# A fourth split tile in the weight ring of a hybrid layer, with the tiles that make room for it

## The chip, the cores and the metric

One Trainium2 chip, one of its cores. The time is device microseconds of one execution. TensorE is called PE, VectorE DVE, ScalarE ACT, GpSimd POOL; SP issues the transfers.

## The reference

One layer of a hybrid trunk for two groups of tokens, 128 context tokens and 256 latent ones, that share the weights: 384 tokens (T) of width 2048 (D), all in float32. Cut to what matters:

```python
mod = silu(c) @ w_mod + b_mod                     # 2048 -> 6 x 2048, one row per group
h   = rmsnorm(x, norm_mix_g) * (1 + sc_a) + sh_a
mq, mk, mv, mo, mi, mf, rq, rk, rv, rg, sz, sxbc, sdt, gl = split(h @ w_in)
y_m = head_rmsnorm(mlstm(mq, mk, mv, mi, mf)) * sigmoid(mo)   # both directions, chunks of 128
y_r = head_rmsnorm(retention(rq, rk, rv)) * silu(rg)          # both directions, rope on the latents
y_s = rmsnorm(ssd(silu(conv(sxbc)), sdt) * silu(sz))          # both directions
g   = sigmoid(gl)                                 # three gates of width 2048
x   = x + g_a * ((g[0]*(y_m @ w_br_m) + g[1]*(y_r @ w_br_r) + g[2]*(y_s @ w_br_s)) @ w_out)
h   = rmsnorm(x, norm_mlp_g) * (1 + sc_f) + sh_f
x   = x + g_f * (square(relu(h @ w_ff1)) @ w_ff2)
y   = rmsnorm(x, final_norm_g)
```

The final states of the three scans of the context group are outputs too.

## The kernel before

**Products.** A float32 operand is split into a rounded part and a remainder (`whi`, `wlo` for weights; `hhi`, `hlo` or `yhi`, `ylo` for activations), and each product is made of three: high by high, high by low, low by high. The weights are read once, in units of 512 KB: a unit is a `raw` tile of 128 x 1024, loaded by SP (`emit_raws`, L139), from which ACT rounds `whi` (L88) and DVE subtracts `wlo` (L91). `raw` tiles come from a ring of `RAWB` = 6, split tiles from a ring of `SPB` = 3. On PE an "A" unit is 24 matmuls of 128 x 384 with the weights stationary, a "B5" unit 18 matmuls with 512 columns of weights moving.

**The main loop.** `run_units` goes through a list of 696 units in program order. For unit i it first emits the splits up to unit i + `SPB` - 1 (`emit_splits`), then loads as far as the ring of raws allows, then the products of unit i, one step of background work (`bg_steps`), some of the modulation's multiplications (`pop_mods`), and at last the evacuation of the block before (`flush_evac`). Each engine works through its own instructions in the order in which they are emitted here. 128 of the units are of kind "M": a tile of `w_mod`, which is no work for PE at that place but is multiplied and summed by ACT, DVE and POOL (L339, L348). They stand among the others in the list, and count as a unit where the ring looks ahead. The background work is the scans, written as generators with a `yield` behind each step: the mLSTM's, the SSD's (`s_scan`, once for each of two groups of heads) and retention's.

**The SSD scan.** `s_scan` works over six pairs n of chunk and direction. `load(n)` brings a tile `Cb` of eight heads' decays (L1004) and, from n = 2, a tile `EB` for the carried state (L1008). `decay(n)` makes exponentials of `Cb` on ACT and DVE, `weigh(n)` multiplies the masked scores into `Cb` on DVE and makes `xd` on POOL, `inter(n)` is the part of the carried state (PE, then `ti` on DVE with `EB`), and `outs(c)` multiplies `xd` and `Cb` of both directions of a chunk on PE. The ring of `Cb` has 5 buffers, that of `EB` 2, and `load(n + 2)` stands at the end of step n. `h0`, the state at the start, has a buffer of its own.

**The start stage**, up to about 205 us, makes the modulation of `h` and the first gate in ten groups of one row tile (the first four) or two. Each group has units of two halves; in a half unit (`st_half`) PE makes 8/n/2 products that ACT, DVE or POOL add to `acc` (for odd products with one row tile by a copy `at` on ACT, L533). `st_split(i + 2)` stands at the beginning of a unit's second half; the next group's work (`st_gemv`: PE's product with `w_mod`; `st_vec`: its turn into columns; `st_build`: `hhi`, `hlo` of the next row tiles) stands behind the halves that the table `nxt` names.

**Retention.** `r_evac_qk`, `r_evac_v` and `r_evac_g` evacuate q and k, v, and the gate of a pair of heads. `yhi` is a tile of eight slots from the pool `hl`; `y_split` fills it, and `y_op` hands it to the products.

The longest part of the run, from about 1760 to 2750 us, is the MLP: nothing but units and the modulation's last tiles.

Of the kernel before, what the change touches and what calls it, by code (L numbers as in the profile page):

```python
# [16 lines left out]
T = 384  # L17
# [29 lines left out]
def hybrid_step(ctx: ExitStack, tc: tile.TileContext, cpack, x_prompt, x_sample, c, state_mlstm_C,  # L47
# [3 lines left out]
                final_norm_g, y_prompt, y_sample, new_C, new_n, new_m, new_ret, new_ssd):  # L51
    nc = tc.nc
    act, dve, pool, pe, sp = nc.scalar, nc.vector, nc.gpsimd, nc.tensor, nc.sync
    RAWB, SPB = 6, 3

    class Pool:
        def __init__(self, name, side="left", space=None):
# [20 lines left out]
    def gbank(name="gb"):  # L78
        return psum([128, 512], name, bufs=4, tag="g")
# [7 lines left out]
    def rnd(out, in_, **kw):  # L87
        act.activation(out=out, in_=in_, func=AF.Copy, **kw)  # L88
# [421 lines left out]
        held["w"] -= 1  # L510
        st_pump()

    def st_half(i, half):
        g, u = units[i]
        k0, n = groups[g]
        if half:
            st_split(i + 2)
        wh, wl = wsp[i]
        nc_ = 8 // n
        for c_ in range(nc_ // 2 * half, nc_ // 2 * half + nc_ // 2):  # L520
            p = gbank()[:, 0:T]
            q = slice(128 * c_, 128 * c_ + 128)
            for kk in range(n):
                k = k0 + kk
                mm(p, wh[:, kk, q], hhi[:, k], kk == 0, False)
                mm(p, wh[:, kk, q], hlo[:, k], False, False)
                mm(p, wl[:, kk, q], hhi[:, k], False, kk == n - 1)
            a = acc[:, nc_ * u + c_]
            if g == 0:
                act.copy(out=a, in_=p)  # L530
            elif n == 1 and c_ % 2:
                t = start([128, T], "at", bufs=2)
                act.copy(out=t, in_=p)  # L533
                tt(pool, a, a, t, ALU.add)
            else:
                tt(dve, a, a, p, ALU.add)
                if g == NG - 1:
                    act.activation(out=a, in_=a, func=AF.Sigmoid)
# [32 lines left out]
    def st_m0(g):  # L571
        st_gemv(g, 0)

    nxt = {1: {0: (st_m1, st_m0), 1: (st_vec,), 2: (st_build,)}, 2: {1: (st_m1,), 3: (st_m0,), 4: (st_vec,), 5: (st_build,)}}
    i = 0
    for g, (k0, n) in enumerate(groups):
        if g == 4:
            vr2, vr3 = start([84, 128], "vr2", tag="vr1"), start([16, 128], "vr3", tag="crow")
            load_later(graw[:, :, 16:48], w_in[0, :, SDT:SDT + 32].rearrange("(k p) f -> p k f", p=128))
            load_later(graw[:, :, 0:16], w_in[0, :, MI:MI + 16].rearrange("(k p) f -> p k f", p=128))  # L580
            load_later(cp[:, CW0:], cpack[:, CW0:CW1])
            for o, n_, v in ((0, 8, m_norm_g[0]), (8, 8, r_norm_g[0]), (16, 8, s_norm_g[0]), (72, 12, s_conv_b[0])):
                load_later(vr2[o:o + n_], rows(v))
            load_later(vr2[24:72], s_conv_w[0].rearrange("w (a b) -> (w a) b", b=128))
            load_later(vr3, state_mlstm_n[0, 0].rearrange("d h (t p) -> (d h t) p", p=128))
            for d in range(2):
                load_later(biasv[32 * d:32 * d + 4], colv(m_igate_b[0, d]))
                load_later(biasv[64 + 32 * d:68 + 32 * d], colv(m_fgate_b[0, d]))
                load_later(biasv[32 * d + 16:32 * d + 32], colv(s_dt_bias[0, d]))
                load_later(alog[32 * d + 16:32 * d + 32], colv(s_a_log[0, d]))  # L590
                load_later(m0[32 * d:32 * d + 4], colv(state_mlstm_m[0, 0, d]))
            load_later(lg, r_decay[0].rearrange("d h -> (d h)").partition_broadcast(128))
            for hf in range(2):
                load_later(sdv[64 * hf:64 * hf + 64, 0:8],
                           s_d[0].rearrange("(t e) -> e t", e=2)[hf].partition_broadcast(64))
        if g == NG - 1:
            take_vectors(vr2, vr3)
        for h_ in range(4 * n):
            if g == NG - 1 and h_ in (4, 6):
                g_prep(h_ // 2 - 2)  # L600
            st_half(i + h_ // 2, h_ % 2)
            if later_loads:
                later_loads.popleft()()
            for f in nxt[n].get(h_, ()):
                f(g + 1)
        i += 2 * n

    def h_op(k):
# [382 lines left out]
    def s_scan(g):  # L991
# [7 lines left out]
        def load(n):  # L999
            if n < 6:  # L1000
                c_, d = cd[n]
                t = Cbs[n] = Ps([128, 8, 128], "Cb", bufs=5)
                r0 = 32 * d + 16 + 8 * g
                sp.dma_start(out=t, in_=scr[2, r0:r0 + 8, 128 * c_:128 * c_ + 128].partition_broadcast(128))  # L1004
                if n >= 2:
                    E = Ebs[n] = Ps([128, 4, 128], "EB", bufs=2)
                    for hf in range(2):
                        sp.dma_start(out=E[64 * hf:64 * hf + 64],  # L1008
                                     in_=scr[1, r0 + hf:r0 + 8:2, 128 * c_:128 * c_ + 128].partition_broadcast(64))

        def decay(n):
            c_, d = cd[n]
# [38 lines left out]
            yo = y_s[:, 4 * g:4 * g + 4, q]  # L1051
            tt(dve, yo, yo, r3(p_, 4), ALU.add)

        h0 = Ps([128, 2, 4, 128], "h0")
        hT = Ps([128, 2, 2, 512], "hT")
        for d in range(2):
            for j in range(4):
# [54 lines left out]
        for n in range(8):  # L1112
            if n >= 3 and n % 2:
                outs((n - 3) // 2)
            if n < 6:
                decay(n)
                yield
            if 1 <= n < 7:
                weigh(n - 1)
                if 2 <= n < 6:  # L1120
                    inter(n)
                yield
            load(n + 2)

    def s_evac_z(j):
        def f(ps):
# [18 lines left out]
    def s_end():  # L1145
        p_ = bank()
        mm(p_[:, 0:T], ones, SS["sqs"])
        run_delayed(True)
        P["s"].close()
        P["hl"] = Pool("hl", "right")  # L1150
        Rs = P["Rs"] = P["hl"]([128, T], "Rs")
        act.activation(out=Rs, in_=p_[:, 0:T], func=AF.Sqrt, scale=1.0 / 1024, bias=K("eps")[:, 0:1])
        dve.reciprocal(out=Rs, in_=Rs)
        P["yhi"] = P["hl"]([128, 8, T], "yhi", dt=F32R)
        P["ylo"] = [None] * 8
        P["r"] = Pool("pr", "right")
        r_begin()
        yield
# [49 lines left out]
    def r_evac_qk(p, which):  # L1208
        def f(ps):
            Pr = P["r"]  # L1210
            r_free(p)
            t = Pr([128, 3, 512], which + "tok")
            act.activation(out=t[:, 0], in_=ps[0], func=AF.Copy, scale=1.0 if which == "q" else 128.0 ** -0.5)
            for c_ in (1, 2):
                cos, sin = (K(n + which)[:, 64 * c_ - 64:64 * c_] for n in ("cos", "sin"))
                for q in (slice(0, 256), slice(256, 512)):
                    t1, t2 = Pr([128, 4, 64], "rt1"), Pr([128, 4, 64], "rt2")
                    s4 = ps[c_][:, q].rearrange("p (a b) -> p a b", b=64)
                    tt(dve, t1, s4, bcast(cos, 1, 4), ALU.mult)
                    tt(dve, t2, s4, bcast(sin, 1, 4), ALU.mult)  # L1220
                    o4 = t[:, c_, q].rearrange("p (h x b) -> p h x b", h=2, x=2)
                    t1v, t2v = (x.rearrange("p (h x) b -> p h x b", x=2) for x in (t1, t2))
                    tt(pool, o4[:, :, 0], t1v[:, :, 0], t2v[:, :, 1], ALU.subtract)
                    tt(pool, o4[:, :, 1], t1v[:, :, 1], t2v[:, :, 0], ALU.add)
            for i in range(2):
                heads.setdefault(2 * p + i, {})[which] = t[:, :, 256 * i:256 * i + 256]
        return f

    def r_evac_v(p):
        def f(ps):  # L1230
            r_free(p)
            t = P["r"]([128, 3, 512], "vtok")
            for c_ in range(3):
                act.copy(out=t[:, c_], in_=ps[c_])
            for i in range(2):
                heads[2 * p + i]["v"] = t[:, :, 256 * i:256 * i + 256]
                bg.append(r_scan(2 * p + i))
        return f
# [106 lines left out]
        yield  # L1345

    def y_split(i, src):
        rnd(P["yhi"][:, i], src)
        if P["ylo"][i] is None:
            P["ylo"][i] = P["hl"]([128, T], "ylo%d" % i, dt=F32R)  # L1350
        tt(dve, P["ylo"][i], src, P["yhi"][:, i].bitcast(F32), ALU.subtract)

    def r_evac_g(p):
        def f(ps):
            while p not in r_done:
                bg_steps(1)
            for i in range(2):
                sg = P["r"]([128, T], "sg", bufs=2)
                act.activation(out=sg, in_=ps[i][:, 0:T], func=AF.Silu)
                tt(pool, sg, sg, RR[2 * p + i], ALU.mult)  # L1360
                later(1, lambda i=i, sg=sg: y_split(2 * p + i, sg))
        return f
# [21 lines left out]


    def y_op(k):
        return P["yhi"][:, k], P["ylo"][k]

    GG = {}

# [357 lines left out]
```

## Time and profile before

| | us |
|---|---|
| median of 3 runs | 2800.89 (2799.49 to 2803.43) |
| the profiled execution, its own time | 2799.41 |
| its span in the trace | 2797.6 |
| PE busy | 2726.8 (97%) |
| DVE busy | 1531.8 (55%) |
| ACT busy | 1122.1 (40%) |
| POOL busy | 638.7 (23%) |

The span is what the trace covers of the profiled execution; the 1.8 us between it and the execution's own time lie around it. Busy time counts the instructions that work, not those that issue transfers or wait. A matmul's record is longer than the distance to the next, since matmuls overlap: what counts is the distance from start to start.

### The profile page before, as it was taken

To read this page: it belongs to the slowest core of one execution; us is meant where nothing else is said; L and a number is where in the kernel's file an instruction comes from. 1 tells how busy PE (TensorE), PEld (TensorE's weight loads), DVE (VectorE), ACT (ScalarE), POOL (GpSimd) and SP (SyncE) were. 2 spreads that over 40 slices of the span, in tenths; PEclk is the share of its full clock that TensorE was granted. 3 is DMA by queue.
4 is the path that set the end of the run, shared out by engine and by line. 5 is a ranking of instruction groups with operands and counts; after the bars stand their busy time and mean duration, and the time that the engine had idled before them with its cause. 6 is when DMAs were issued, how large, how long until landed. Compare 5 with 4: busy or idle time off the path is not lost. (4 is left out here: it accounts for less than half of the span.)

```text
span 2797.6 us, 38171 instructions
## 1 busy us (share of the span) xinstructions
PE 2726.8 (97%) x15109; PEld 2509.8 (90%) x15109; DVE 1531.8 (55%) x1937; ACT 1122.1 (40%) x1656; POOL 638.7 (23%) x534
## 2 busy tenths in 40 slices
PE   8999999999999999999999998999999999999998
PEld 7899989898888888999999987998899899889987
DVE  3666566666546556667558646767334334334434
ACT  5333454546543342443344445544233233323333
POOL 4200233402241111121236422345100100010012
PEclk9999999999999999999999999999999999999999
DMA  9955456466646455666656743666443444344442
GB/s 318 314 187 172 139 174 180 133 184 184 184 120 195 149 168 160 182 180 196 205 183 215 255 155 91 194 190 194 139 128 127 130 128 125 128 130 126 126 144 102
DMA packets 381755, 471.03 MB, mean 168 GB/s; under 512 B 21317, under 2 KB 281049, under 8 KB 380425
## 3 DMA queue, kind: packets, MB, share of 16 engines
q1 hardware_dynamic: 381576, 468.61, 54.2%
q8 instruction: 118, 1.93, 0.3%
q14 instruction: 61, 0.49, 0.1%
HBM read 452.22 MB, written 16.33 MB: 167 GB/s over the span
## 5 line engine op out<-in xcount | busy, mean ns | idle before, releaser
L91 DVE TENSOR_TENSOR wlo<-raw,whi 128x1024 fp32r<-128x1024 f32 x599 | 799.8, 1340 | 953.4 <-ACT whi L88 951.9
L88 ACT ACTIVATE whi<-raw 128x1024 fp32r<-128x1024 f32 x600 | 631.9, 1058 | 987.9 <-PE gb L100 446.3
L100 PE MATMUL gb<-hhi,whi 128*128 128x384 f32 x1600 | 551.4, 345 | 11.3 <-ACT whi L88 5.9
L100 PE MATMUL gb<-hhi,wlo 128*128 128x384 f32 x1600 | 540.0, 337 | 16.7 <-DVE wlo L91 16.5
L100 PE MATMUL gb<-hlo,whi 128*128 128x384 f32 x1600 | 537.4, 336 | 0.4 <-DVE hlo L91 0.4
L100 PE MATMUL gb<-h2l,whi 128*128 128x384 f32 x1024 | 344.5, 336 | 5.1 <-DVE h2l L1555 5.0
L100 PE MATMUL gb<-h2i,whi 128*128 128x384 f32 x1024 | 343.9, 336 | 1.5 <-ACT h2i L1551 1.5
L100 PE MATMUL gb<-h2i,wlo 128*128 128x384 f32 x1024 | 343.4, 335 | 0.0
L100 PEld LDWEIGHTS gb<-hhi,whi 128*128 128x128 f32 x1600 | 302.2, 189 | 27.0 <-issue 9.3
L339 DVE SCALAR_TENSOR_TENSOR macc<-raw,cs,macc 128x512 f32<-128x512 f32 x372 | 319.4, 872 | 7.6 <-DMA macc<-in_b_mod_dram 0.7
L100 PEld LDWEIGHTS gb<-hhi,wlo 128*128 128x128 f32 x1600 | 301.9, 189 | 23.1 <-DVE wlo L91 22.9
L100 PEld LDWEIGHTS gb<-hlo,whi 128*128 128x128 f32 x1600 | 302.0, 189 | 1.7 <-DVE hlo L91 0.7
L91 POOL TENSOR_TENSOR macc<-macc,raw 128x512 f32<-128x512 f32 x140 | 224.7, 1605 | 335.2 <-issue 283.4
L91 POOL TENSOR_TENSOR x<-x,t 128x512 f32<-128x512 f32 x45 | 71.6, 1621 | 735.6 <-DVE t L91 735.6
L100 PEld LDWEIGHTS gb<-h2l,whi 128*128 128x128 f32 x1024 | 193.2, 189 | 8.0 <-DVE h2l L1555 7.9
L100 PE MATMUL gb<-whi,ahi 128*128 128x512 f32 x512 | 199.4, 389 | 0.0
L100 PE MATMUL gb<-whi,alo 128*128 128x512 f32 x512 | 199.3, 389 | 0.0
L100 PE MATMUL gb<-wlo,ahi 128*128 128x512 f32 x512 | 199.2, 389 | 0.0
L100 PEld LDWEIGHTS gb<-h2i,whi 128*128 128x128 f32 x1024 | 193.3, 189 | 2.9 <-ACT h2i L1551 1.9
L100 PEld LDWEIGHTS gb<-h2i,wlo 128*128 128x128 f32 x1024 | 193.3, 189 | 0.0
L100 PE MATMUL gb<-ylo,whi 128*128 128x384 f32 x384 | 128.4, 334 | 0.6 <-DVE ylo L91 0.6
L100 PE MATMUL gb<-yhi,whi 128*128 128x384 f32 x384 | 128.5, 335 | 0.0
(443 smaller groups left out, 3872.7 us busy)
## 6 DMA issues: line engine op xcount, KB each, us to landing
raw<-in_w_in_dram SPq DMA_DIRECT2D x264, 512.0 KB
raw<-in_w_ff_dram SPq DMA_DIRECT2D x256, 512.0 KB
raw<-in_w_mod_dram SPq DMA_DIRECT2D x128, 512.0 KB
mraw<-in_w_mod_dram SPq DMA_DIRECT2D x32, 1024.0 KB
raw<-in_w_out_dram SPq DMA_DIRECT2D x32, 512.0 KB
sg<-scr_g SPq DMA_DIRECT2D x22, 384.0 KB
raw<-in_w_br_r_dram SPq DMA_DIRECT2D x16, 512.0 KB
raw<-in_w_br_m_dram SPq DMA_DIRECT2D x16, 512.0 KB
```

The source lines that it names most:

```text
L88: act.activation(out=out, in_=in_, func=AF.Copy, **kw)
L91: eng.tensor_tensor(out=out, in0=a, in1=b, op=op)
L100: pe.matmul(out, l, r, start=start, stop=stop)
L339: dve.scalar_tensor_tensor(out=macc[:, v], in0=t[:, kk], scalar=cs[:, 2 * r + kk, v:v + 1], in1=macc[:, v], op0=ALU.mult, op1=ALU.add)
```

## The change

The split ring gets a fourth tile of each kind, 8 KB more in a partition. Room comes from three places: the decay tiles `Cb` go from five buffers to four, which `h0` shares, and are loaded two at a time at odd n (for n = 3 behind `outs(0)`); `EB` goes from two buffers to one, loaded behind the `inter` that read it last; and `qtok` and `vtok` of retention take the two buffers in which `yhi` stands later, now as two tiles of four slots, made when the first gate is evacuated. In the start stage the next group's work and the split move from the ends of half units into their middle, and `st_build` in the groups with two row tiles from behind half unit 5 into half unit 6. No engine gets an instruction more or less.

```diff
-    RAWB, SPB = 6, 3
+    RAWB, SPB = 6, 4
...
-    def st_half(i, half):
+    def st_half(i, half, mid):
         g, u = units[i]
         k0, n = groups[g]
-        if half:
-            st_split(i + 2)
         wh, wl = wsp[i]
         nc_ = 8 // n
         for c_ in range(nc_ // 2 * half, nc_ // 2 * half + nc_ // 2):
+            if c_ % (nc_ // 2) == nc_ // 4:
+                for f in mid:
+                    f(g + 1)
+                if half:
+                    st_split(i + 2)
             p = gbank()[:, 0:T]
...
-    nxt = {1: {0: (st_m1, st_m0), 1: (st_vec,), 2: (st_build,)}, 2: {1: (st_m1,), 3: (st_m0,), 4: (st_vec,), 5: (st_build,)}}
+    nxt = {1: {0: (st_m1, st_m0), 1: (st_vec,), 2: (st_build,)}, 2: {1: (st_m1,), 3: (st_m0,), 4: (st_vec,), 6: (st_build,)}}
...
-            st_half(i + h_ // 2, h_ % 2)
+            st_half(i + h_ // 2, h_ % 2, nxt[n].get(h_, ()))
             if later_loads:
                 later_loads.popleft()()
-            for f in nxt[n].get(h_, ()):
-                f(g + 1)
...
-                t = Cbs[n] = Ps([128, 8, 128], "Cb", bufs=5)
+                t = Cbs[n] = Ps([128, 8, 128], "Cb", bufs=4)
                 r0 = 32 * d + 16 + 8 * g
                 sp.dma_start(out=t, in_=scr[2, r0:r0 + 8, 128 * c_:128 * c_ + 128].partition_broadcast(128))
-                if n >= 2:
-                    E = Ebs[n] = Ps([128, 4, 128], "EB", bufs=2)
-                    for hf in range(2):
-                        sp.dma_start(out=E[64 * hf:64 * hf + 64],
-                                     in_=scr[1, r0 + hf:r0 + 8:2, 128 * c_:128 * c_ + 128].partition_broadcast(64))
+
+        def load_e(n):
+            if 2 <= n < 6:
+                c_, d = cd[n]
+                r0 = 32 * d + 16 + 8 * g
+                E = Ebs[n] = Ps([128, 4, 128], "EB")
+                for hf in range(2):
+                    sp.dma_start(out=E[64 * hf:64 * hf + 64],
+                                 in_=scr[1, r0 + hf:r0 + 8:2, 128 * c_:128 * c_ + 128].partition_broadcast(64))
...
-        h0 = Ps([128, 2, 4, 128], "h0")
+        h0 = Ps([128, 2, 4, 128], "h0", bufs=4, tag="Cb")
...
             if n >= 3 and n % 2:
                 outs((n - 3) // 2)
+            if n % 2:
+                load(n + 1)
+                if n == 1:
+                    load_e(2)
+                load(n + 2)
             if n < 6:
                 decay(n)
                 yield
...
                 if 2 <= n < 6:
                     inter(n)
+                    load_e(n + 1)
                 yield
-            load(n + 2)
...
-        P["yhi"] = P["hl"]([128, 8, T], "yhi", dt=F32R)
...
-            t = Pr([128, 3, 512], which + "tok")
+            t = P["hl"]([128, 3, 512], "qtok", bufs=2, tag="yhi") if which == "q" else Pr([128, 3, 512], "ktok")
...
-            t = P["r"]([128, 3, 512], "vtok")
+            t = P["hl"]([128, 3, 512], "vtok", bufs=2, tag="yhi")
...
-        rnd(P["yhi"][:, i], src)
+        yh = P["yhi"][i // 4][:, i % 4]
+        rnd(yh, src)
...
-            while p not in r_done:
+            while p not in r_done or not {2, 3} <= r_read:
                 bg_steps(1)
+            if p == 0:
+                P["yhi"] = [P["hl"]([128, 4, T], "yhi", bufs=2, dt=F32R) for _ in range(2)]
```

How the order moves. First ACT, some units into the main loop, where the first scan of the mLSTM ends; `whi` are the splits, L348 multiplies tiles of the modulation, L905 (L906 in the changed kernel) writes the mLSTM's output. Before:

```order
L893 ACTIVATE jk,sq<-hb 128x256
L88 ACTIVATE whi<-raw 128x1024
L895 ACT_TABLE_LOAD
L895 ACTIVATE sq<-sq,cp 128x3
L88 ACTIVATE whi<-raw 128x1024 x2
L348 ACTIVATE raw<-raw,cs 128x512 x2
L905 ACTIVATE y_m<-sb,vec 128x384 x2
L348 ACTIVATE raw<-raw,cs 128x512 x2
L88 ACTIVATE whi<-raw 128x1024 x2
L792 COPY v_3984<-gb 128x2x256 x2
```

And now:

```order
L894 ACTIVATE jk,sq<-hb 128x256
L88 ACTIVATE whi<-raw 128x1024
L896 ACT_TABLE_LOAD
L896 ACTIVATE sq<-sq,cp 128x3
L88 ACTIVATE whi<-raw 128x1024
L348 ACTIVATE raw<-raw,cs 128x512 x2
L88 ACTIVATE whi<-raw 128x1024
L906 ACTIVATE y_m<-sb,vec 128x384 x2
L88 ACTIVATE whi<-raw 128x1024
L348 ACTIVATE raw<-raw,cs 128x512 x2
L88 ACTIVATE whi<-raw 128x1024
L793 COPY v_3988<-gb 128x2x256 x2
```

Between the two pairs of L348 stood no split, and two behind them; now one stands behind the first pair, one behind `y_m`, one behind the second pair.

SP's queue in the second scan, from the stores of `so` on; L1105, L1004, L1008 and L1178 are L1110, L1005, L1013 and L1187 in the changed kernel. Before:

```order
L1105 DMA out_dram<-so 128x128 x8
L1004 DMA Cb<-scr 128x8x128
L1008 DMA EB<-scr 64x4x128 x2
L139 DMA raw<-in_w_in_dram 128x4x256
L1178 DMA scr_g<-ga__6941 128x384
L1178 DMA scr_g<-ga__6943 128x384
L1004 DMA Cb<-scr 128x8x128
L1008 DMA EB<-scr 64x4x128 x2
L1004 DMA Cb<-scr 128x8x128
L1008 DMA EB<-scr 64x4x128 x2
L139 DMA raw<-in_w_in_dram 128x4x256 x5
```

And now:

```order
L1110 DMA out_dram<-so 128x128 x8
L1005 DMA Cb<-scr 128x8x128
L1013 DMA EB<-scr 64x4x128 x2
L1005 DMA Cb<-scr 128x8x128
L1187 DMA scr_g<-ga__6949 128x384
L1187 DMA scr_g<-ga__6951 128x384
L1013 DMA EB<-scr 64x4x128 x2
L1005 DMA Cb<-scr 128x8x128 x2
L139 DMA raw<-in_w_in_dram 128x4x256 x6
L1187 DMA scr_g<-ga__7132 128x384
L1187 DMA scr_g<-ga__7134 128x384
L1013 DMA EB<-scr 64x4x128 x2
```

The loads of `Cb` come in pairs, and of the loads of `EB` (two halves each) the third now comes behind the raws that it stood ahead of.

ACT in the start stage, around a copy of the modulation (L461), a build (L490 and `hhi`) and the `at` copies (L533, now L536). Before:

```order
L461 COPY macc<-gemv 128x256
L88 ACTIVATE whi<-raw 128x1024
L533 COPY at<-gb 128x384 x4
L490 ACTIVATE ht<-sb,shA,scA 128x128
L490 ACTIVATE ht<-sb,shA,scA 128x256
L88 ACTIVATE hhi<-ht 128x384
L88 ACTIVATE whi<-raw 128x1024
L533 COPY at<-gb 128x384 x4
L461 COPY macc<-gemv 128x256
L88 ACTIVATE whi<-raw 128x1024
```

And now:

```order
L461 COPY macc<-gemv 128x256
L536 COPY at<-gb 128x384 x2
L88 ACTIVATE whi<-raw 128x1024
L536 COPY at<-gb 128x384 x2
L490 ACTIVATE ht<-sb,shA,scA 128x128
L490 ACTIVATE ht<-sb,shA,scA 128x256
L88 ACTIVATE hhi<-ht 128x384
L536 COPY at<-gb 128x384 x2
L88 ACTIVATE whi<-raw 128x1024
L536 COPY at<-gb 128x384 x2
L461 COPY macc<-gemv 128x256
```

The copies stood in fours, with build and split one behind the other; now they stand in pairs, one of the other things between each two.

## Rows read from the trace of the kernel before

**Rows 1.** Page: busy time; xcount | busy, mean ns | idle before it.

```profile
PE 2726.8 (97%) x15109; PEld 2509.8 (90%) x15109; DVE 1531.8 (55%) x1937; ACT 1122.1 (40%) x1656; POOL 638.7 (23%) x534
...
L91 DVE TENSOR_TENSOR wlo<-raw,whi 128x1024 fp32r<-128x1024 f32 x599 | 799.8, 1340 | 953.4 <-ACT whi L88 951.9
L88 ACT ACTIVATE whi<-raw 128x1024 fp32r<-128x1024 f32 x600 | 631.9, 1058 | 987.9 <-PE gb L100 446.3
```

**Rows 2.** Windows: us, busy PE, PEld, DVE, ACT, POOL, PEclk, DMA, GB/s.

```profile
340.00:650.00 310.00, 300.82 (x1663) 282.02 (x1662) 197.53 (x282) 153.92 (x255) 103.69 (x104) 1.00 0.56 167
650.00:1075.00 425.00, 400.24 (x2242) 364.07 (x2241) 249.86 (x331) 186.50 (x297) 101.64 (x104) 0.98 0.56 164
1760.00:2750.00 990.00, 990.00 (x5046) 903.25 (x5045) 451.46 (x452) 344.16 (x426) 161.44 (x98) 1.00 0.46 143
```

**Rows 3.** Waits of PE, 340 to 1265 us: total, times, longest.

```profile
PE gb L100 <- DVE wlo L91: 25.4, 22, 2.9
PE gb L100 <- ACT whi L88: 6.6, 4, 3.5
PE sb L100 <- POOL xd L91: 3.5, 1, 3.5
```

**Rows 4.** Timeline of ACT: start, us, operation xcount [idle before <-releaser].

```profile
413.10 1.33 ACT L348 ACTIVATE raw<-raw,cs 128x512 f32<-128x512 f32 x2
414.32 2.00 ACT L88 ACTIVATE whi<-raw 128x1024 fp32r<-128x1024 f32 x2
```

**Rows 5.** Timeline of PE behind two of the waits.

```profile
417.77 0.45 PE L100 MATMUL gb<-hhi,wlo 128*128 128x384 f32 x1 [0.88 <-DVE wlo L91]
...
1258.19 0.33 PE L100 MATMUL gb<-hlo,whi 128*128 128x384 f32 x1
1259.74 0.44 PE L100 MATMUL gb<-hhi,wlo 128*128 128x384 f32 x1 [1.21 <-DVE wlo L91]
```

**Rows 6.** Timeline of PE, 657 to 662 us.

```profile
657.56 0.44 PE L100 MATMUL gb<-hhi,wlo 128*128 128x384 f32 x1 [2.36 <-DVE wlo L91]
...
658.01 0.52 PE L100 MATMUL gb<-hlo,whi 128*128 128x384 f32 x1
...
661.21 0.42 PE L100 MATMUL gb<-hhi,wlo 128*128 128x384 f32 x1
```

**Rows 7.** Windows at three stretches of lower clock (PEclk third from end).

```profile
657.00:662.00 5.00, 4.44 (x16) 4.45 (x17) 1.66 (x6) 4.97 (x10) 0.00 (x0) 0.66 0.39 105
808.00:812.00 4.00, 3.48 (x30) 3.18 (x31) 0.13 (x1) 0.90 (x2) 3.37 (x4) 0.57 0.48 136
1067.00:1071.00 4.00, 2.90 (x7) 2.32 (x8) 3.96 (x6) 1.25 (x2) 2.42 (x3) 0.57 0.44 123
```

**Rows 8.** Timelines of SP and ACT: a load, and who waits for it.

```profile
1024.04 0.93 SPq L139 DMA_DIRECT2D raw<-in_w_in_dram  x2
...
1028.70 1.06 ACT L88 ACTIVATE whi<-raw 128x1024 fp32r<-128x1024 f32 x1 [0.72 <-DMA raw<-in_w_in_dram]
```

**Rows 9.** Waits of PE, 0 to 340 us.

```profile
PE gb L100 <- ACT at L533: 3.6, 3, 1.8
```

**Rows 10.** Timelines of SP and ACT, second scan; waits of SP.

```profile
750.13 0.38 SPq L1004 DMA_DIRECT2D Cb<-scr  x1
...
754.49 1.28 ACT L1017 ACTIVATE Cb<-Cb,colA 128x128 f32<-128x128 f32 x4 [5.73 <-DMA Cb<-scr]
...
777.94 0.45 SPq L1004 DMA_DIRECT2D Cb<-scr  x1
...
785.23 1.28 ACT L1017 ACTIVATE Cb<-Cb,colA 128x128 f32<-128x128 f32 x4 [0.18 <-DMA Cb<-scr]
...
SPq L1008 <- DVE ti L91: 7.2, 2, 4.8
```

**Rows 11.** Waits of PE, 650 to 810 us.

```profile
PE gb L100 <- DVE wlo L91: 5.4, 4, 2.4
PE gb L100 <- ACT whi L88: 5.4, 2, 3.5
```

More of the change, by code (lines that the diff above doesn't have):

```diff
@@ L1347, in y_split @@
     def y_split(i, src):
-        rnd(P["yhi"][:, i], src)
+        yh = P["yhi"][i // 4][:, i % 4]
+        rnd(yh, src)
         if P["ylo"][i] is None:
             P["ylo"][i] = P["hl"]([128, T], "ylo%d" % i, dt=F32R)
-        tt(dve, P["ylo"][i], src, P["yhi"][:, i].bitcast(F32), ALU.subtract)
+        tt(dve, P["ylo"][i], src, yh.bitcast(F32), ALU.subtract)
     def r_evac_g(p):
         def f(ps):
-            while p not in r_done:
+            while p not in r_done or not {2, 3} <= r_read:
                 bg_steps(1)
+            if p == 0:
+                P["yhi"] = [P["hl"]([128, 4, T], "yhi", bufs=2, dt=F32R) for _ in range(2)]
             for i in range(2):
@@ L1386, in y_op @@
     def y_op(k):
-        return P["yhi"][:, k], P["ylo"][k]
+        return P["yhi"][k // 4][:, k % 4], P["ylo"][k]
     GG = {}
```

## The prediction

> **What bounds the kernel now.** The page comes first: PE is busy for 97% of the span, DVE for 55%, ACT for 40% [rows 1]. So only two things can shorten the run: PE's gaps, and stretches in which PE runs at its lower clock. The windows by stage then show where the gaps are [rows 2]: from 340 to 1075 PE lacks 9.2 and 24.8 us, while from 1760 to 2750 it is busy for 990.00 of 990 us, although the same ring of three split tiles feeds it there. The ring is too short only where other work shares ACT and DVE with it (DVE is busy for 64% from 340 to 650, for 46% from 1760 on).
>
> The waits of PE name the gaps [rows 3]: from 340 to 1265 it waits 22 times for `wlo` (25.4 us) and 4 times for `whi` (6.6 us), once for `xd` (3.5 us). ACT's timeline shows how one arises [rows 4]: two `whi` start at 414.32, right behind multiplications of the modulation's tiles (L348) from 413.10; the subtraction on DVE (1.34 us, [rows 1]) can only follow, and PE goes on at 417.77 [rows 5]. These raws had long landed; the split stood too late in ACT's own order. In the kernel's order, 239 real units of the main loop have but one other real unit between the emission of their split and its use (where a unit of the modulation, which gives PE nothing, takes the place of the second), and all but one of the small waits fall on such units.
>
> A wait costs more than its idle [rows 5]: from 1258.19 to 1259.74 are 1.55 us between two starts that are otherwise 0.17 apart, and only 1.21 of them are idle: 0.16 more for the refill. Last, the clock [rows 6]: behind the wait of 2.36 us at 657.56 the matmuls start 0.32 us apart instead of 0.17, from 658.01 to 661.21; the granted clock of that stretch is 0.66 of full, the lower level, 1.2 of 2.4 GHz, for two thirds of it [rows 7]. There are six such stretches from 650 to 1075, the last at 1067; five follow a wait for a split, the one at 808 the wait for `xd`.
>
> **The change part by part.**
>
> a) *The ring, 3 to 4.* Every split is issued one unit earlier on ACT and DVE. In the new order 222 of the 239 units have two real units in between, 17 still one. One A unit is 24 matmuls at 0.173 = 4.15 us of PE; the longest wait for a split is 3.5 us [rows 3]. So one unit covers each of the waits, if the split moves by its whole unit. The waits are 25.4 + 6.6 = 32.0 us over 26 times, with the refill 32.0 + 26 x 0.16 = 36.2 us. Of these 17/239 stay, 2.6, and I keep 0.6 back for units that gain less than their whole lead: **-33.0 us**. What pays: the raw is wanted a unit earlier. The one landing that shows in full takes 4.66 us, from the issue at 1024.04 to 1028.70 [rows 8]; with `whi` 1.06 and `wlo` 1.34 [rows 1] it makes 7.1 us from issue to use. Two A units are 8.3 us, so I take it as covered (rival B, if not).
>
> b) *The clock.* In that stretch ten steps take 3.20 us where they would take 1.73: 1.5 us lost [rows 6]. Five of six stretches follow a split wait: 5 x 1.5 = **-7.5 us**. Between 0 (the lower level comes for another reason) and -9.
>
> c) *The start stage* (0 to about 205). Vectors, gemv, build and split move from the ends of half units into their middles. PE's waits there for the `at` copies are 3.6 us, three times [rows 9]; the copy now stands ahead of the split in three of the groups with one row tile (1 us of ACT, the length of `whi`), so I take 3 x 1.0 saved, against 1.0 in the first group and some 0.6 where the build now comes half a unit later and is followed at once by its use: **-1**, between -6 (all of the 3.6 with refills, and a little of the gemv's) and +4 (four of the groups lose one `whi` each).
>
> d) *The decay tiles.* The `Cb` ring goes from 5 to 4 and is shared with `h0`; tiles come in pairs, and the second pair's loads wait on SP for PE's `outs`. `EB` has one buffer: its next load waits until DVE has made `ti`. Such waits of SP exist already, 7.2 us over 2 [rows 10]. Behind SP's wait stand raw loads; they were issued many units ahead, and 7 us of delay is not yet seen by PE while raws are two units ahead. A `Cb` lands in 4.36 us (750.13 to 754.49, with ACT idle for 5.73) or at most 7.29 (777.94 to 785.23) [rows 10]; between a load of `EB` and its use stand two background steps, so two units, 8.3 us. By that it is covered, with a margin of 1.0 us. I take **+2**, between 0 and +8 (two holds of the upper kind with half of it covered). "Double-buffer for performance" is a rule of the Trainium skill (page Trainium Kernel Development and Optimization, section Best Practices), so that transfers overlap with compute. It speaks against the single buffer of `EB`; by it each load would stand bare, which is rival D.
>
> e) *`xd`.* The wait for it is untouched (POOL works it, behind ACT's exponentials) and PE arrives there sooner, as the waits ahead of it are gone: **+1.1**, between 0 and +3.5 (as much again, [rows 3]).
>
> f) *What is late next.* Background steps on PE wait for DVE and ACT, which now work nearer to PE. DVE's 64% rises to some 66% when the stretch shortens. From 1760 to 2750 nothing is late [rows 2], so the lower end is 0; the upper is three waits of the longest `wlo` kind, 3 x (2.9 + 0.16) = 9.2, say 10. I take **+2**.
>
> `qtok` and `vtok` in the ring of `yhi` cost nothing: the gate's evacuation now also waits for two more reads, and in the emission no background step has to be forced for them; covered by the steps already made. If that cover went, one step more (4.2 us) would come early, not in addition.
>
> Sum: -33.0 - 7.5 - 1 + 2 + 1.1 + 2 = -36.4 us. The profiled execution took 2799.4 us (span 2797.6 and 1.8 around it): 2763.0. The median of the runs shown is 1.5 above the profiled one, so **2764.5 us**.
>
> **The rivals.**
>
> *B, raws come late.* The raws' own ring stays at six, so a longer split ring takes its unit out of the lead of the raws: in the new order 82 splits, not 29, come right behind the issue of their raw. If each of the 53 more makes ACT wait as at 1028.70, 0.72 us [rows 8], ACT loses 38 us, and what is queued behind it waits too; with half of it on PE, +19: 2764.5 + 19 = 2783. For: the landing is there in the row. Against: ACT is idle for 60% and the margin to use is two units.
>
> *C, nothing moves.* ACT's splits are held by PE anyway: before `whi` ACT was idle for 446.3 us because PE still read the tile [rows 1]. If the ring's length only moves where ACT stands, and each split still meets the same work ahead of it, about 2800. For: the 446 us. Against: they belong mostly to stretches where PE lacks nothing; and by the order, the split of rows 4 moves ahead of the multiplications that held it.
>
> *D, slower: the single `EB` and the pairs.* Each scan makes four loads with no spare buffer (`EB` of 3, 4 and 5, `Cb` of 4), eight for two scans. If what waits for them holds up ACT and DVE for a whole landing, 7.29 us [rows 10], and the splits queued behind, PE loses 8 x 7.3 = 58 us. The stage's own split waits (10.8 us, six times, [rows 11]) and clock stretches would remain, so the gain elsewhere is 32.0 - 10.8 + 20 x 0.16 = 24.4 and two stretches, 3.0. 2799.4 + 58.4 - 27.4 = 2830.4, with the 1.5 **2832 us**. It decides from (27.4 + 5.6)/8 = 4.1 us per hold. For: ACT did wait 5.73 us for a `Cb`. Against: two units lie between.
>
> **How the numbers follow.** A, the sum, 0.73; B 0.17; C 0.06; D 0.04. A's own range is 2752 (clock and start at their good ends, nothing late) to 2782 (c, d, e and f at their bad ends: 5 + 6 + 2.4 + 8 = 21, of which not all at once). The range reaches over B: **2752 to 2786**, which leaves out C, D and a tenth of the rest. About 0.2% (5.6 us) can be told from no change: faster 0.90 (A and B), same 0.06 (C), slower 0.04 (D).
>
> **What would show it.** Right: waits for `wlo` and `whi` from 340 to 1265 under 5 us in all; one clock stretch, behind `xd`; PE's idle from 71 to about 40 us; 1760 to 2750 as before. Wrong: `whi` waiting for DMA of raw often (B); the same waits for `wlo` at other places (C); ACT, DVE or PE waiting for `EB` or `Cb` by DMA, more than 4 us eight times over (D); a stretch at 1.2 GHz without a wait ahead of it (term b).

## The result, and the profile after

The changed kernel takes **2759.93 us** (median of 4 runs, 2758.89 to 2761.18) against 2800.19 (4 runs, 2798.99 to 2803.43) for the kernel before: a ratio of 0.9855, 95% interval 0.9838 to 0.9872. That is 40.3 us less; the forecast was 36.4 less, and 2764.5.

First the page of the changed kernel (parts 1 and 5, as [rows 1]):

```profile
span 2757.7 us, 38218 instructions
...
PE 2714.7 (98%) x15109; PEld 2508.3 (91%) x15109; DVE 1522.9 (55%) x1937; ACT 1122.0 (41%) x1656; POOL 627.0 (23%) x534
...
L88 ACT ACTIVATE whi<-raw 128x1024 fp32r<-128x1024 f32 x600 | 629.8, 1057 | 931.2 <-PE sb L100 385.9
```

PE's work is the same 15109 matmuls; its idle time falls from 70.8 to 43.0 us, and its busy time from 2726.8 to 2714.7 although nothing was taken from it: the longer matmuls at the lower clock and the 0.16 us that a wait costs beyond its idle [rows 5] both count as busy. ACT still idles in front of `whi` for PE, 385.9 us where matmuls into the tiles `sb` release it and 381.2 where those into `gb` do; before it was 445.5 and 446.3, and the page's line in [rows 1] shows only the larger of the two. Next the waits of PE from 225 to 1240 us, the stretch that answers to [rows 3]; columns are total us, times, longest:

```profile
PE sb L100 <- POOL xd L91: 4.8, 2, 3.7
PE sb L100 <- DVE Cb L91: 4.7, 4, 1.9
PE gb L100 <- DVE wlo L91: 1.5, 3, 0.7
```

The 26 waits for splits, 32.0 us, have become three, 1.5 us. In their place stand four waits for `Cb` (0.4 us before) and two for `xd` (one, 3.5). The windows by stage, which answer to [rows 2], and the one stretch at the lower clock that is left between the start stage and the MLP ([rows 7] for those of before):

```profile
339.00:636.30 297.30, 297.30 (x1667) 283.37 (x1666) 194.37 (x282) 155.08 (x257) 103.09 (x104) 1.00 0.58 173
636.30:1039.00 402.70, 391.56 (x2242) 358.06 (x2241) 246.35 (x327) 184.58 (x296) 98.11 (x103) 0.99 0.57 172
1720.00:2710.00 990.00, 990.00 (x5046) 903.27 (x5045) 448.23 (x451) 344.00 (x425) 155.68 (x98) 1.00 0.45 143
783.00:791.00 8.00, 4.65 (x33) 4.32 (x34) 3.67 (x4) 0.90 (x2) 7.37 (x7) 0.57 0.39 125
```

From 339 to 636 PE now lacks nothing of 297.30 us (before: 9.2 of 310); in the next stage 11.1 (24.8); in the MLP the same 990.00 of 990. The six stretches at 1.2 GHz from 650 to 1075 have become one, from 783.8 on, 6.83 us long; it begins within the second of the two waits for `xd` (782.6 to 786.35). The stretch at the MLP's beginning, behind waits for `x` and `h2i`, is there in both kernels (from 1716 for 13.7 us before, from 1678 for 17.1 now), and the start stage has a new one (below). These are the signs that the prediction asked for: under 5 us of waits for splits, one stretch, behind `xd`, about 40 us of idle, the MLP as before.

How the split of [rows 4] now stands on ACT:

```profile
405.99 1.51 ACT L348 ACTIVATE raw<-raw,cs 128x512 f32<-128x512 f32 x2 [3.96 <-DVE macc L339]
409.65 1.06 ACT L88 ACTIVATE whi<-raw 128x1024 fp32r<-128x1024 f32 x1 [2.15 <-PE sb L104]
410.61 1.03 ACT L906 ACTIVATE y_m<-sb,vec 128x384 f32<-128x384 f32 x2
411.54 1.06 ACT L88 ACTIVATE whi<-raw 128x1024 fp32r<-128x1024 f32 x1
412.66 1.51 ACT L348 ACTIVATE raw<-raw,cs 128x512 f32<-128x512 f32 x2
414.08 1.04 ACT L88 ACTIVATE whi<-raw 128x1024 fp32r<-128x1024 f32 x1
```

The `whi` run singly, one behind the first pair of multiplications (409.65), one behind `y_m` (411.54), one behind the second pair (414.08). Before, two of them started at 414.32, and PE waited 0.88 us [rows 5]; now nothing on PE waits there.

### The profile page after: what moved, and what is told of

Its sections match the earlier page's. It is cut to its first block, busy times and chain, and to the rows that moved or that the text cites. A ratio compares the mean times of both kernels' runs of the same rounds, so it can differ in the third digit from the quotient of the medians.

```text
span 2757.7 us, 38218 instructions
## 1 busy us (share of the span) xinstructions
PE 2714.7 (98%) x15109; PEld 2508.3 (91%) x15109; DVE 1522.9 (55%) x1937; ACT 1122.0 (41%) x1656; POOL 627.0 (23%) x534
## 4 chain that ended last, share of the span: by engine, by line
PE 86%; DVE 2%; issue 1%; ACT 1%; DMA 1%; POOL 0%; SPq 0%; DVEq 0%; ACTq 0%; POOLq 0%
PE gb L100 70%; PE sb L100 15%; PE sb L104 1%; DMA raw<-in_w_in_dram 1%; DVE wlo L91 0%; DVE h2l L1567 0%; ACT whi L88 0%; DVE macc L339 0%; DVE Cb L91 0%; POOL y_s L91 0%; POOL y_s L1152 0%; DVE x L91 0%; DMA Cb<-scr 0%; POOL xd L91 0%; ACT h2i L1563 0%
## 5 line engine op out<-in xcount | busy, mean ns | idle before, releaser
L88 ACT ACTIVATE whi<-raw 128x1024 fp32r<-128x1024 f32 x600 | 629.8, 1057 | 931.2 <-PE sb L100 385.9
L339 DVE SCALAR_TENSOR_TENSOR macc<-raw,cs,macc 128x512 f32<-128x512 f32 x372 | 303.7, 829 | 12.2 <-DMA macc<-in_b_mod_dram 2.9
```

The costliest lines, as they stand in the source:

```text
L339: dve.scalar_tensor_tensor(out=macc[:, v], in0=t[:, kk], scalar=cs[:, 2 * r + kk, v:v + 1], in1=macc[:, v], op0=ALU.mult, op1=ALU.add)
```

## The experiments

Times are medians. They stand beside the changed kernel's 2759.93 and, as ratios, beside runs of the kernel before on the same chip (medians 2800.73, 2801.57 and 2801.51 us).

**Is it the ring?** The ring back at three:

```diff
-    RAWB, SPB = 6, 4
+    RAWB, SPB = 6, 3
```

> The changed kernel with the ring of split tiles back at 3, all else as changed. Theory R (the ring pays for everything): the waits for wlo and whi and the stretches at 1.2 GHz come back, 36 and 6 us, and the waits for Cb and xd that the change brought shrink by 2 to 5 us, as PE comes later to them: 2797 to 2803 us. Theory S (the moved order of scans and start stage carries a third or more): below 2787.

Measured: 2799.32 us, ratio to before 0.9995 (0.9986 to 1.0003). Waits of PE, 225 to 1265:

```profile
PE gb L100 <- DVE wlo L91: 24.7, 22, 2.9
PE gb L100 <- ACT whi L88: 6.3, 4, 3.2
PE sb L100 <- POOL xd L91: 3.5, 1, 3.5
PE sb L100 <- DVE Cb L91: 0.4, 1, 0.4
```

Theory R. With three tiles all else in the change is worth nothing that can be measured, and it costs nothing either: with pairs of `Cb`, one `EB` and the new start the waits for `Cb` and `xd` are those of before to a tenth.

**Is it the tile or its place in the order?** Four tiles, but each split emitted where three tiles had it:

```diff
-            emit_splits(i + SPB)
+            emit_splits(i + SPB - 1)
```

> Four split tiles as changed, but a split is emitted at the index at which three tiles had it (one unit later). Theory O (what counts is the place in ACT's and DVE's order; PE's hold on the tile does not matter): the time of the ring of 3, within 5 us, with 20 or more waits for wlo. Theory T (what counts is that the tile is free earlier): within 5 us of the changed kernel, 2755 to 2765.

Measured: 2797.11 us, ratio 0.9988 (0.9980 to 0.9997). ACT's timeline at the place of [rows 4]:

```profile
412.13 1.33 ACT L348 ACTIVATE raw<-raw,cs 128x512 f32<-128x512 f32 x2
413.36 2.00 ACT L88 ACTIVATE whi<-raw 128x1024 fp32r<-128x1024 f32 x2
```

The waits of PE there, 225 to 1265 us:

```profile
PE gb L100 <- DVE wlo L91: 25.0, 23, 2.9
PE gb L100 <- ACT whi L88: 6.6, 4, 3.5
```

Theory O. The pair of `whi` is back behind the multiplications, and the waits for splits with it. A free tile alone gives about 2 us; what the fourth tile is good for is that it allows the split to be put one unit earlier into the queues of ACT and DVE.

**What is the start stage worth?** `st_half`, `nxt` and the loop of the start as before, the rest as changed:

```diff
-                for f in mid:
-                    f(g + 1)
-                if half:
-                    st_split(i + 2)
...
+        if half:
+            st_split(i + 2)
...
+            for f in nxt[n].get(h_, ()):
+                f(g + 1)
```

> The changed kernel with the start stage as before. If the start stage is a zero sum by its waits (copies give 2.4 us, the gemv's load costs 1.6, a new stretch at 1.2 GHz near 30 us costs 3.4): within 1.5 us of the changed kernel, no stretch near 30 us, waits for at copies back at 3.6 us. If the moved order was worth something of its own: 2763 or more; if the stretch is all it brings: 2757 or less.

Measured: 2762.60 us (2760.28 to 2763.24), ratio 0.9861 (0.9846 to 0.9876). The new order is worth 2.7 us by the medians and 1.7 by the ratios (0.9861 and 0.9855). That lies between the first two theories, and the intervals overlap. The waits for the `at` copies are back at 3.5 us, as expected, but two stretches of lower clock appeared at other places (windows, PEclk third from the end):

```profile
21.00:26.00 5.00, 4.51 (x52) 4.24 (x45) 0.47 (x4) 2.86 (x6) 1.39 (x1) 0.71 1.01 268
83.00:88.00 5.00, 4.71 (x18) 4.71 (x19) 3.92 (x6) 2.53 (x4) 4.68 (x4) 0.66 1.08 358
```

The kernel before, with the same order in this stage, had none there; another run with that order (four of each, below) has them from 22 and from 83.5 us on. So what the start stage gives depends in part on stretches whose place the order doesn't set; that stays open.

**Why does PE now wait for `Cb` and `xd`?** `outs(1)` and `outs(2)` one background step later:

```diff
-            if n >= 3 and n % 2:
-                outs((n - 3) // 2)
+            if n == 3:
+                outs(0)
+            elif n == 7:
+                yield
+                outs(2)
...
             if 1 <= n < 7:
+                if n == 5:
+                    outs(1)
                 weigh(n - 1)
```

> The changed kernel with outs(1) and outs(2) of the SSD scan one background step later. Theory L (PE now arrives at outs before weigh and xd are done, one unit is enough): the waits for Cb at 680 and 698 (2.1 and 1.7 us with refill) and for xd at 780 and 782 (5.1) go, and with the last the stretch at 1.2 GHz near 784 (3.1): 2748 us, 2745 to 2752. If the stretch comes without a wait ahead of it: 2751 to 2754. If weigh and xd are simply pushed along with the step (DVE and POOL are behind for more than one unit): 2757 to 2762.

Measured: **2748.09 us** (2747.82 to 2748.41), ratio 0.9812 (0.9799 to 0.9826), the lowest time found, with one other that can't be told apart from it (below). Its waits of PE, 225 to 1265 us:

```profile
PE gb L100 <- DVE wlo L91: 2.1, 4, 0.7
PE sb L100 <- DVE Cb L91: 0.4, 1, 0.4
```

Theory L, with the time worked out for it. Both waits for `xd` and three of four for `Cb` are gone, and no stretch at 1.2 GHz is left between the start stage and the MLP. At the same place as before, around the `outs` that start at 784.43 without a wait, the granted clock (third from the end) is now 1.00:

```profile
783.00:791.00 8.00, 7.99 (x66) 7.33 (x65) 2.90 (x2) 1.25 (x3) 6.99 (x5) 1.00 0.43 129
```

So the stretch at 783.8 came with the waits for `xd`.

**Or do the single `EB` and the pairs hold the scan up?** First two buffers for `EB`:

```diff
-                E = Ebs[n] = Ps([128, 4, 128], "EB")
+                E = Ebs[n] = Ps([128, 4, 128], "EB", bufs=2)
```

> The changed kernel with two buffers for EB (its next load no longer waits for ti). Theory F (PE's new waits for Cb come from PE being earlier, not from the loads): the four waits for Cb, 4.7 us, and the two for xd, 4.8 us, stay, DVE's 1.1 us for EB goes: 2758 to 2761. Theory D (the single buffer holds SP, and what stands behind it): the waits for Cb fall below 2 us, 2752 to 2757.

Measured: 2759.48 us, ratio 0.9851 (0.9835 to 0.9867). Waits of PE:

```profile
PE sb L100 <- DVE Cb L91: 5.2, 4, 1.9
PE sb L100 <- POOL xd L91: 4.8, 2, 3.7
```

Then `Cb` loaded one at a time, in the ring of four:

```diff
-            if n % 2:
-                load(n + 1)
-                if n == 1:
-                    load_e(2)
-                load(n + 2)
+            if n == 3:
+                load(4)
+            if n == 1:
+                load_e(2)
...
                 yield
+            if n != 2:
+                load(n + 2)
```

> The changed kernel with the tiles Cb loaded one at a time again, at the ends of steps 0, 1 and 3 and (that of n = 4) behind outs(0), in the same ring of four. Theory F (PE's new waits come from PE being earlier): waits for Cb 4 to 6 us in 4, for xd 4.8 in 2, 2758 to 2762. Theory P (the pairs hold up SP, ACT or DVE): the waits for Cb fall under 2 us, 2752 to 2757.

Measured: 2759.81 us, ratio 0.9854 (0.9840 to 0.9867); `xd` 4.8 us in 2, `Cb` 3.5 in 3. Both times theory F by the time and by `xd`; the waits for `Cb` without pairs came out somewhat below its 4 to 6 us in 4. Neither the single buffer nor the pairs cost anything that the time shows. The loads have enough ahead of them, although SP in the changed kernel waits longer for `ti` than before (7.2 us in 2, [rows 10]):

```profile
SPq L1013 <- DVE ti L91: 16.8, 5, 6.0
```

**How much lead have the raws left?** Five raws:

```diff
-    RAWB, SPB = 6, 4
+    RAWB, SPB = 5, 4
```

> The changed kernel with five raws instead of six. In it ACT waits 27 times, 77 us in all, for a raw to land (before: 7 times, 16.9 us), and PE sees none of it. Theory M (behind these waits lies more than a unit of reserve, 4.15 us): no wait of PE for whi or wlo above 1 us, 2763 at most. Theory N (less than a unit lies there, so the change has used up the lead of the raws): ten or more of the 27 reach PE with 1 to 4 us each, 2770 to 2790.

Measured: 2768.97 us, ratio 0.9884 (0.9869 to 0.9899): 9.0 slower than the change, between the two theories. ACT's timeline shows a wait for a raw:

```profile
553.32 1.06 ACT L88 ACTIVATE whi<-raw 128x1024 fp32r<-128x1024 f32 x1 [6.10 <-DMA raw<-in_w_in_dram]
```

and PE's timeline what comes of it:

```profile
554.43 0.69 PE L100 MATMUL gb<-hhi,whi 128*128 128x384 f32 x1 [3.85 <-ACT whi L88]
...
556.49 0.52 PE L100 MATMUL gb<-hlo,whi 128*128 128x384 f32 x1
...
560.65 0.52 PE L100 MATMUL gb<-hhi,wlo 128*128 128x384 f32 x1
```

One raw (not ten) reaches PE late, by 3.85 us, and behind it the matmuls start 0.32 us apart for some 6 us: the one wait costs about twice its idle. The rest of the 9.0 goes with it in small waits: `Cb` 6.7 us in 5 (4.7 in 4 before), `wlo` 2.4 in 6 (1.5 in 3). In the rest of the 49 waits of ACT for a raw PE doesn't wait over 1 us for a split, so for all but one the reserve is more than a unit, and for that one less.

**The same ring paid by the raws.** The kernel before with four of each:

```diff
-    RAWB, SPB = 6, 3
+    RAWB, SPB = 4, 4
```

> The kernel before with four split tiles paid by two raws (six to four), all else as before. If the split's place in the order is all that counts: 2760, as changed. If the lead of the raws is as short as theory N has it: two units less cost twice what five raws cost, 2785 to 2830, waits of PE for whi behind DMA of raw.

Measured: 2824.37 us, ratio 1.0078 (1.0063 to 1.0093), slower than before. ACT's wait for raws from 225 to 1240 us:

```profile
ACT whi L88 <- DMA raw<-in_w_in_dram: 186.3, 64, 18.2
```

and waits of PE, for `wlo` from 225 to 1265 us and from 1300 us on, and for the gemv's loads:

```profile
PE gb L100 <- DVE wlo L91: 7.8, 8, 2.5
...
PE gb L100 <- DVE wlo L91: 8.2, 8, 1.8
...
PE gemv L100 <- DMA mraw<-in_w_mod_dram: 10.1, 7, 2.7
```

From 225 to 1265 us two thirds of the wait for `wlo` are away (25.4 to 7.8), but new waits stand there, the longest of 5.3 us for `kT` and 4.1 for `Cb`. The start loses 11 us (there the loads stand in one line, and that of a raw that has to wait holds the next ones), and the MLP, where nothing was late in the kernel before, waits for splits and loses 13 (both by where the same matmuls stand in the two traces: 222.7 against 211.7 us at the end of the start, 25.7 later at the MLP's end against 12.3 at its beginning). The unit of lead has to come from elsewhere than the raws, and that is what the smaller tiles of the scans pay for.

**The first group of the start as before, with `outs` later.**

```diff
-            st_half(i + h_ // 2, h_ % 2, nxt[n].get(h_, ()))
+            st_half(i + h_ // 2, h_ % 2, nxt[n].get(h_, ()) if g else ())
...
+            if g == 0:
+                for f in nxt[n].get(h_, ()):
+                    f(g + 1)
```

> The changed kernel with outs(1) and outs(2) one step later and, in the first group of the start stage, the next group's work at the ends of half units as before. If the gemv's wait for its load (2.5 us near 28) is what the middle costs and what the stretches at 1.2 GHz near 14 and 30 follow: both go, 2744 to 2746. If these stretches come without regard to that order (as in the start stage put back as before, which had two): 2747 to 2749.

Measured: 2747.74 us, ratio 0.9808 (0.9793 to 0.9823), not told apart from 2748.09: the second value. The gemv's waits for its loads come to 4.8 us against 3.3, but in the eight traces with the start stage as changed they lie anywhere from 3.3 to 5.2, so nothing follows from that. One stretch at 1.2 GHz stands in the first 100 us (from 22 on), where the version above has two (from 14 and from 31).

**All three `outs` later**, with the loads that stand behind the first:

```diff
             if 1 <= n < 7:
+                if n in (3, 5):
+                    outs((n - 3) // 2)
+                if n == 3:
+                    load(4)
+                    load(5)
                 weigh(n - 1)
```

> The changed kernel with all three outs one step later, and the loads of Cb 4 and 5 behind outs(0), so one step later too. The waits for Cb left in front of outs(0) cost 1.8 us: if the loads have a unit to spare, 2746 to 2747.5. If the landing (4.4 to 7.3 us against one unit of 4.15) now holds ACT at decay(4) and the splits behind it: 2749 to 2757.

Measured: 2755.21 us (2754.11 to 2756.62), ratio 0.9837 (0.9824 to 0.9851), 7 slower than with `outs(0)` in its place. SP's timeline in the first scan:

```profile
661.00 12.24 SPq L139 DMA_DIRECT2D raw<-in_w_in_dram  x5
673.33 1.48 SPq L1005 DMA_DIRECT2D Cb<-scr  x2
```

ACT's:

```profile
679.55 1.28 ACT L1022 ACTIVATE Cb<-Cb,colA 128x128 f32<-128x128 f32 x4 [8.19 <-PE gb L100]
```

and PE's, with `outs(0)` and what comes later:

```profile
661.81 1.97 PE L100 MATMUL sb<-Cb,xd 128*64 128x128 f32 x32
...
683.01 0.44 PE L100 MATMUL gb<-hhi,whi 128*128 128x384 f32 x1 [3.33 <-ACT whi L88]
```

The second value, but not by the landing alone. PE was done with `outs(0)` at 663.8; SP stood until 673 in front of raws that were emitted ahead of the two loads, and only then issued them. ACT's `decay` starts at 679.55, after 8.19 us of idle (put down to PE, which had long been done), and the `whi` queued behind it comes 3.33 us late to PE. This is rival D's mechanism at work, in another place, and the one hold costs about what D took for each of its eight, 7.3 us.

## Why the prediction was right

**The ring (a)** was the right term and a little small: -33.0 forecast. Counted from start to start of the matmuls, each distance less the median of its kind, the 26 waits for splits cost 36.6 us before and the three 2.0 after, so -34.6. Of the 3.2 us that the forecast let stand (2.6 and 0.6), 2.0 stood. The mechanism is shown twice: by the ring of three, and by four tiles in the old order.

**The clock (b)**: -7.5 forecast; the matmuls that start late in these stretches, without those that waited, lose 10.0 us before and 2.6 after, -7.4. That the stretch follows a wait was argued from five cases; the version with `outs` later, which removes the last long wait and the last stretch together, supports it. The six stretches cost 1.7 us each where the forecast took 1.5; which wait brings one isn't settled (last section).

**The start (c)**: -1 forecast. In the two profiles PE reaches the end of this stage 0.3 us sooner; the copies' waits fall from 3.6 to 1.2 us, the gemv's are 5.2 instead of 3.6 (other runs with this order have as little as 3.3, so the order isn't shown to raise them), and a stretch at 1.2 GHz appears that I hadn't foreseen. Eleven of the twelve traces of this case have one or more from 10 to 100 us, with either order; only that of the kernel before has none. Waits of PE, 0 to 225 us, and the window of that stretch (granted clock 0.57):

```profile
PE gemv L100 <- DMA mraw<-in_w_mod_dram: 5.2, 4, 2.5
...
PE gb L100 <- ACT at L536: 1.2, 1, 1.2
```

```profile
29.00:37.00 8.00, 6.28 (x49) 5.80 (x50) 0.00 (x0) 2.13 (x5) 0.00 (x0) 0.57 1.13 322
```

By the runs the new order is worth up to 2.7.

**The decay tiles, `xd` and what is late next (d, e, f)**: +5.1 in all forecast, +6.4 found (counted in the same way, `Cb` 0.60 to 5.66, `xd` 3.74 to 5.06). The sum came out near, but by luck: term d, the loads, is zero (two buffers for `EB`, single loads of `Cb`) where it had +2, and f is +5.1 where it had +2. The two errors cancel in part. What f names, background steps of PE that wait for DVE, is what the trace shows, at two and a half times the size. At 682.72 PE waits for the product `Cb` x `cbm` on DVE, which stands behind a split there, and at 782 and 786 for POOL's `xd`. DVE's and PE's timelines:

```profile
680.22 1.23 DVE L91 TENSOR_TENSOR wlo<-raw,whi 128x1024 fp32r<-128x1024 f32 x1 [1.65 <-ACT whi L88]
681.36 1.22 DVE L91 TENSOR_TENSOR Cb<-Cb,cbm 128x1024 f32<-128x1024 f32 x1
```

```profile
682.72 1.75 PE L100 MATMUL sb<-Cb,xd 128*64 128x128 f32 x28 [1.91 <-DVE Cb L91]
...
782.17 0.44 PE L100 MATMUL sb<-Cb,xd 128*64 128x128 f32 x4 [1.01 <-POOL xd L91]
...
786.35 3.25 PE L100 MATMUL sb<-Cb,xd 128*64 128x128 f32 x28 [3.75 <-POOL xd L91]
```

The splits came earlier and freed PE; `outs`, one unit behind `weigh`, then came before its operands.

The terms as measured make -34.6 - 7.4 - 0.3 + 6.4 = -35.9 of the 39.9 us between the spans of the two profiled executions; the rest, 4.0, lies in small gaps that I don't assign.

**Rival B** was half right, and its sign would have misled me. ACT did come to wait for raws, as it said. Waits of ACT from 225 to 1240, before and after:

```profile
ACT whi L88 <- PE sb L100: 101.5, 34, 7.8
ACT whi L88 <- PE gb L100: 50.2, 21, 3.4
ACT whi L88 <- DMA raw<-in_w_in_dram: 16.9, 7, 5.0
```

```profile
ACT whi L88 <- DMA raw<-in_w_in_dram: 77.0, 27, 10.4
ACT whi L88 <- PE sb L100: 56.7, 21, 4.9
ACT whi L88 <- PE gb L100: 48.3, 19, 3.1
```

That is 60 us more, where B had 38. But PE's waits for splits went to 1.5 us. ACT's idle time in front of `whi` was 152 us for PE and 17 for raws; now it is 105 and 77: one idle took the place of the other, and behind it stands the added unit of lead. The step "half of it on PE" was the wrong one. The run with five raws shows how near the edge this is: one unit less and the first raw is late on PE.

**Rival C** (the splits are held by PE anyway) falls with the four tiles in the old order: there the tile is free earlier and the time hardly moves (2797.11 us). **Rival D** didn't come about: with two units between load and use, one buffer was enough, and a second one gave nothing. The rule weighed there (the Trainium skill, page Trainium Kernel Development and Optimization, section Best Practices: overlap transfers with compute by two buffers) speaks of the overlap, and the measurement differs from reading it as a second tile: 2759.48 us with two buffers, 2759.93 with one. The distance in the order gave the overlap.

## What to carry to other kernels

When an engine that is 97% busy waits for short preparations by other engines that are half idle, look at the order in their queues, not at their load: a longer ring helps as far as it puts the preparation ahead of the work that delays it. Ask what pays for the lead (here not the raws, which had a reserve of hardly more than a unit), and then look at what was just in time before: PE came sooner to `outs` than DVE and POOL to its operands, and moving that consumer by one step gave 12 us more, for nothing. A move is free only where no load is tied to it: moving `outs(0)`, behind which two loads then stand in a queue of raws, gave 7 back.

## What the runs showed of the hardware that I had not expected

A wait on PE can cost twice its idle: 3.85 us in the run with five raws, and 0.32 instead of 0.17 us between matmuls from 554.9 to 560.9 behind it. Every stretch at the lower clock in the twelve traces, from 10 us on and but for the one at the run's end, begins within a wait of PE or less than 2.5 us behind one, in the start stage too. But not each wait brings one, and the same wait brings it in one run and not in another. PE waited 1.77 us for an `at` copy in the kernel before (until 81.83) and the granted clock stayed at 1.00; it waited 1.77 us there with the start stage put back (until 83.29), and a stretch begins at 84.5. It waited 2.39 us for `wlo` in the kernel before (until 1035.12), with no stretch behind it, and 2.36 at that place with four tiles in the old order (until 1034.02), with one from 1034.9 on. No run here tells what decides.
